# Transposes of the gate-up product tied behind later branch blocks, a last up stage in two branches, and paired down rows

## The chip, the cores and the metric

The kernel runs on one core of one Trainium2 chip. The metric is device time in microseconds of one execution; the median of several executions counts.

## The reference

A two-layer network on 256 tokens of width 1024, all in fp32. Layer 0 has a gated delta-rule mixer and a dense SwiGLU, layer 1 a windowed attention and a mixture of experts. The change touches the mixture alone:

```python
def moe_swiglu(x, w_router, w_gate, w_up, w_down):
    ...
    top_val, top_idx = lax.top_k(logits, TOP_K)          # TOP_K = 2 of 8 experts
    top_w = jax.nn.softmax(top_val, axis=-1)
    gates = jnp.einsum('nk,nke->ne', top_w, jax.nn.one_hot(top_idx, N_EXPERTS))
    for e in range(N_EXPERTS):
        h = jax.nn.silu(xf @ w_gate[e]) * (xf @ w_up[e])  # 1024 -> 3584
        out = out + gates[:, e:e + 1] * (h @ w_down[e])   # 3584 -> 1024
```

## The kernel before

The experts run one after another, each on up to 128 gathered tokens. An expert's 3584 hidden columns are cut into seven blocks b of 512. The weights come from HBM in units of 1 MB (128 partitions x 2048 fp32), 42 units an expert: two for each of gate, up and down of each block. `unit` (L140 to L158) issues the load on SP's queue into a ring of raw buffers, lets ScalarE cast it to the short form hi (L154) and VectorE subtract to get the rest lo (L155). There are four buffers each for hi and lo.

TensorE then multiplies. In the three-product arm (`mm3`, L167) each weight column block is used as hi with the tokens' hi and lo part and as lo with the hi part; the two-product arm (`mm2`, L1202) packs hi and lo of up to 64 tokens into one operand, uses each weight twice, and adds the halves with a matmul against `fold` (`addlow`, L1194). `arms` (L1184) puts both arms into a branch on TensorE, which takes the first when the expert has over 64 tokens; expert 0 always takes the first, with no branch. In this run experts 0, 2, 3 and 5 take three products, the others two.

The order is a list of stages (L1296 to L1302). For the blocks of an expert in groups (0, 1), (2, 3), (4, 5), (6): gate of each block, up of each block, then down of the blocks of the group before, then "held". After the last up of a group ScalarE takes silu of the gate sum into `msg`. "held" adds the halves of up in the two-product arm; its other arm is empty. `multiply` (L1327) makes msg times up on VectorE and puts the result into the list `held`; `turn_one` takes one from there to `turned` (L1250): four transposes on TensorE into a bank of `tr` (two banks), ScalarE's copy to the hi half of `hT` (L1256), VectorE's difference (L1257), and, from expert 1 on, ScalarE's two packing copies to `hp` (L1118, L1119). Down of a block reads hT in the one arm, hp in the other.

The framework orders each engine's instructions by itself: it simulates the engines and takes, of what would be ready, what was traced first. A branch block counts as one piece. `tc.issue_after(ins)` puts instructions of the engine of `ins` behind it in the order and adds no wait.

The main loop (L1333) decides where `multiply` and `turn_one` are traced: multiply after gate of an even block, but in "held" for the group (4, 5); turn_one after gate of an odd block or of block 6, and after each up. In the trace the transposes of experts 1 to 7 stand mostly directly behind the held block, between the two down blocks of a group, and those of expert 0 behind gate and up stages.

Of the kernel before, what the change touches and what calls it, by code (L numbers as in the profile page):

```python
# [30 lines left out]
P = 128  # L31
D = 1024
# [7 lines left out]
NE = 8  # L40
# [42 lines left out]
def kernel(ctx: ExitStack, tc: tile.TileContext, A, out):  # L83
    nc = tc.nc
# [12 lines left out]
    ident = per.tile([P, P], F32, name="ident")  # L97
# [42 lines left out]
    def unit(src, a, b, pieces=1):  # L140
        raw = next(raws[0])()
        n = a * b
        for c in range(pieces):
            w = slice(c * b // pieces, (c + 1) * b // pieces)
            nc.sync.dma_start(raw[:, :n].rearrange("p (a b) -> p a b", a=a)[:, :, w], src[:, :, w])
        hi = split.tile([P, 2048], F32R, name="hi", tag="hi")
        lo = split.tile([P, 2048], F32R, name="lo", tag="lo")
        nq = quanta[0]
        with ExitStack() as late:
            if behind[0] is not None:  # L150
                late.enter_context(tc.issue_after(behind[0].ins))
            for q in range(nq):
                c = slice(q * n // nq, (q + 1) * n // nq)
                S.copy(hi[:, c], raw[:, c])  # L154
                subs.append(V.tensor_sub(lo[:, c], raw[:, c], hi[:, c].bitcast(F32)))  # L155
        return (hi[:, :n].rearrange("p (a b) -> p a b", a=a), lo[:, :n].rearrange("p (a b) -> p a b", a=a))
# [931 lines left out]
    with ExitStack() as mctx:  # L1088
# [92 lines left out]
        NB = EF // 512  # L1181
        acc, flags = {}, {}
        y = []
        def arms(e, heavy, light):  # L1184
            if e == 0:
                return heavy()
            if e not in flags:
                flags[e] = nc.values_load(cntsi[0:1, e:e + 1], engines=(mybir.EngineType.PE,), min_val=0, max_val=T)
            with tc.If(flags[e] > HALF) as c:  # L1189
                heavy()  # L1190
            with c.Else():
                light()

        def addlow(ps, low):  # L1194
            PE.matmul(ps, fold, low, start=False, stop=True, skip_group_check=True)
# [8 lines left out]
            for i, w in enumerate(ws[0] + ws[1]):  # L1204
                PE.matmul(ps, x[:, (k0 + i % n) * P:(k0 + i % n + 1) * P], w, start=first and i == 0, stop=last and i == 2 * n - 1)  # L1205

        def gateup(e, b, us, ps, then=lambda: None):

            x = xg[e].rearrange("p l k c -> p l (k c)")
            nk, k0 = (4, 0) if len(ps) == 1 else (2, 4 * (b % 2))  # L1210
            first, last = (len(ps) == 1 or b % 2 == n for n in range(2))

            def parts():
                for u, ws in enumerate(us):
                    for h, p in enumerate(ps):
                        yield p, k0 + nk * u, [[w[:, k, h * 512:(h + 1) * 512] for k in range(nk)] for w in ws], \
                            first and u == 0, last and u == 1

            def heavy():
                for p, k1, (wh, wl), a, z in parts():  # L1220
                    mm3(p, lambda k: x[:, 0, (k1 + k) * P:(k1 + k + 1) * P], lambda k: x[:, 1, (k1 + k) * P:(k1 + k + 1) * P],
                        list(zip(wh, wl)), a, z)

            def light():
                for p, k1, ws, a, z in parts():
                    mm2(p, xp[e], k1, ws, a, z)
                then()
            arms(e, heavy, light)
# [20 lines left out]

        def turned(s, e):  # L1250
            p = trb()
            for f in range(4):
                PE.transpose(p[:, f * P:(f + 1) * P], s[:, f * P:(f + 1) * P], ident)  # L1253
            hT = mp.tile([P, 2, 512], F32R, name="hT", tag="hT")
            hp = mp.tile([P, 512], F32R, name="hp", tag="hp") if e else None
            S.copy(hT[:, 0], p)  # L1256
            V.tensor_sub(hT[:, 1], p, hT[:, 0].bitcast(F32))  # L1257
            if e:
                packed(hp, p, hT[:, 1])
            return hT, hp  # L1260
# [44 lines left out]
        def loads(what, e, b):  # L1305
            if what == "down":
                behind[0] = None
                v = wd_[e].rearrange("(f p) n -> p f n", p=P)
                return [unit(v[:, 4 * b + 2 * u:4 * b + 2 * u + 2, :], 2, D) for u in range(2)]
            w = (wg_ if what == "gate" else wu_)[e]  # L1310
            behind[0] = placed if (e, b) == (0, 1) or (e, b, what) == (0, 0, "up") else None
            if b == NB - 1:
                return colunits(w, 512 * b, 512)
            k0, c0 = 4 * (b % 2), 1024 * (b // 2)
            v = w.rearrange("(k p) n -> p k n", p=P)
            return [unit(v[:, k0 + 2 * u:k0 + 2 * u + 2, c0:c0 + 1024], 2, 1024) for u in range(2)]
# [6 lines left out]
        def turn_one():  # L1323
            e, b, s = held.pop(0)
            hT[e, b] = turned(s, e)

        def multiply():  # L1327
            for bb, pu, _, s_, ee in mine:
                V.tensor_mul(s_, s_, pu)  # L1329
                held.append((ee, bb, s_))  # L1330
            mine.clear()

        for what, e, b in stages:  # L1333
            if what != "held":
                nxt = next(nexts, None)
                quanta[0] = 1 if e or b > 1 else 4
                if nxt:
                    ready[nxt] = loads(*nxt)
                us = ready.pop((what, e, b))
            whole = b == NB - 1 or b % 2  # L1340
            if what == "gate":
                if b % 2 == 0:
                    pgs = [mm() for _ in range(1 if whole else 2)]
                gateup(e, b, us, pgs)
                if b % 2 == 0 and b < NB - 1:
                    multiply()
                elif held:
                    turn_one()
                if whole:
                    lgs_ = [low(p) if e else None for p in pgs]  # L1350
                if kept is not None and (e, b) == (kept[0] + 1, 2):
                    next(kept[1], None)
                    kept = None
            elif what == "up":
                if b % 2 == 0:
                    pus = [up() for _ in range(1 if whole else 2)]
                gateup(e, b, us, pus, lambda: [addlow(p, l) for p, l in zip(pgs, lgs_)] if whole else None)
                if held:
                    turn_one()
                if whole:  # L1360
                    for n, (pg, pu) in enumerate(zip(pgs, pus)):
                        s_ = mp.tile([P, 512], F32, name="msg", tag="msg")
                        S.activation(s_, pg, AF.Silu)
                        mine.append((b - len(pgs) + 1 + n, pu, low(pu) if e else None, s_, e))
                if b == 1 and e + 1 < NE:
                    fetch(e + 1)
                if b == 5 - 2 * (e > 0) and e + 1 < NE:
                    xg[e + 1] = gather(e + 1)
            elif what == "held":
                if e:  # L1370
                    arms(e, lambda: None, lambda: [addlow(pu, lu_) for _, pu, lu_, _, _ in mine])
                if b == NB - 2 or (e, b) == (NE - 1, NB - 1):
                    multiply()
                if (e, b) == (NE - 1, NB - 1):
                    turn_one()
                if (e, b) == (NE - 2, NB - 1):
                    turns.remove(ylng[0])
                    yy = per.tile([P, 2, D], F32, name="y", tag="Bh")
                    for tb in range(2):
                        y.append(yy[:, tb])  # L1380
                        nc.gpsimd.dma_start(y[tb], x3d[tb * P:(tb + 1) * P])
                        G.tensor_scalar(y[tb], y[tb], ALPHA, None, op0=OP.mult)
                if e == NE - 1 and b > 1:
                    with tc.issue_after(subs[-1].ins):
                        for c in late:
                            next(c, None)
                    late = [collect(b // 2 - 1, tb) for tb in range(2)] if b < NB - 1 else []
                    for c in late:
                        next(c)
                if (e, b) == (NE - 1, 1):  # L1390
                    turns.remove(ylng[1])
                    lnp = ln_params(3, nc.gpsimd)
                if (e, b) == (NE - 1, 5):
                    onehot(e, True)
            else:
                down(e, b, hT.pop((e, b)), us)
                if b == NB - 1 and e < NE - 1:
                    kept = (e, keep(e))
                    next(kept[1])
# [104 lines left out]
```

## Time and profile before

| | us |
|---|---|
| median of 3 runs | 1416.77 (1416.58 to 1417.6) |
| profiled execution | 1412.96 |
| its span in the trace | 1411.3 |
| the eight experts in it | about 475 to 1393 |

The page gives the busy share of each engine over the whole span. The trace can be asked for busy time by stretch (windows), for who waited for whom (waits) and for the instructions in order of time (timeline). PE is TensorE, DVE VectorE, ACT ScalarE. A matmul's end is modelled and overlaps the next one's start; the pace of matmuls is read from their starts.

### The profile page before, as it was taken

How to read it: one execution, taken by the hardware profiler on the slowest of the kernel's cores; microseconds unless marked ns; L12 is line 12 of the kernel's file. 1: busy time of each engine (PE TensorE's matmuls, PEld its weight loads, DVE VectorE, ACT ScalarE, POOL GpSimd, SP SyncE). 2: the span in 40 equal slices, each digit the busy share in tenths (PEclk: the TensorE clock that was granted, in tenths of full speed). 3: DMA queues.
4: the chain of work that ended last, by engine and by line, in shares of the span. 5: the costliest groups of instructions: out<-in, count | busy, mean ns of one | idle time of the engine just before them, and what ended most of it. 6: DMA issues, size and time to landing. Idle time of an engine off the chain costs nothing. (4 is left out here: it accounts for less than half of the span.)

```text
span 1411.3 us, 17398 instructions
## 1 busy us (share of the span) xinstructions
PE 1309.4 (93%) x6175; PEld 1042.5 (74%) x6175; DVE 1165.8 (83%) x1300; ACT 1013.4 (72%) x1264; POOL 67.3 (5%) x90
## 2 busy tenths in 40 slices
PE   7999999999999999988999999998989999888884
PEld 5889788888777888766677777776667776666662
DVE  4885975554877898889988888889998889999998
ACT  4763544444364577799888878789988888998983
POOL 4000000000000320000000000000000000002110
PEclk9999999999999899999999999999999999999998
DMA  8641576764643899999999999999999999999992
GB/s 272 199 151 61 180 260 220 236 209 151 203 174 117 306 421 415 362 397 404 419 410 378 353 368 359 359 372 409 405 419 416 357 375 380 395 414 418 419 416 80
DMA packets 145378, 446.76 MB, mean 317 GB/s; under 512 B 12704, under 2 KB 20032, under 8 KB 145264
## 3 DMA queue, kind: packets, MB, share of 16 engines
q1 hardware_dynamic: 137072, 420.64, 78.3%
q0 software_dynamic: 5280, 18.66, 3.5%
q10 hardware_dynamic: 2912, 5.90, 1.3%
q8 instruction: 76, 1.25, 0.3%
q14 instruction: 38, 0.31, 0.1%
HBM read 435.05 MB, written 15.36 MB: 319 GB/s over the span
## 5 line engine op out<-in xcount | busy, mean ns | idle before, releaser
L155 DVE TENSOR_TENSOR lo<-raw,hi 128x2048 fp32r<-128x2048 f32 (+1 forms) x610 | 910.2, 1534 | 115.8 <-ACT hi L154 111.8
L154 ACT CAST hi<-raw 128x2048 fp32r<-128x2048 f32 (+1 forms) x610 | 769.5, 1312 | 152.5 <-PE acc L171 59.1
L1205 PE MATMUL acc<-lo,xp 128*128 128x512 f32 x224 | 74.6, 420 | 18.7 <-DVE lo L155 16.4
L170 PE MATMUL acc<-hi,hT 128*128 128x512 f32 x224 | 88.4, 395 | 2.0 <-ACT hi L154 2.0
L170 PE MATMUL mm<-hi,xg 128*128 128x512 f32 x224 | 87.5, 392 | 0.5 <-ACT low L1199 0.5
L170 PE MATMUL acc<-hi,xg 128*128 128x512 f32 x224 | 88.0, 393 | 0.0
L171 PE MATMUL mm<-hi,xg 128*128 128x512 f32 x224 | 87.3, 390 | 0.0
L171 PE MATMUL acc<-hi,hT 128*128 128x512 f32 x224 | 87.3, 390 | 0.0
L171 PE MATMUL acc<-hi,xg 128*128 128x512 f32 x224 | 87.2, 389 | 0.0
L1205 PE MATMUL mm<-lo,xp 128*128 128x512 f32 x224 | 70.7, 403 | 10.2 <-DVE lo L155 10.1
L1205 PE MATMUL acc<-lo,hp 128*128 128x512 f32 x224 | 71.5, 400 | 4.5 <-DVE lo L155 4.4
L1205 PEld LDWEIGHTS acc<-lo,xp 128*128 128x128 f32 x224 | 38.8, 190 | 45.1 <-DVE lo L155 39.1
L1205 PE MATMUL acc<-hi,hp 128*128 128x512 f32 x224 | 70.7, 397 | 1.2 <-ACT hp L1119 1.2
L1205 PE MATMUL mm<-hi,xp 128*128 128x512 f32 x224 | 68.7, 393 | 2.2 <-ACT low L1199 1.5
L1205 PE MATMUL acc<-hi,xp 128*128 128x512 f32 x224 | 69.7, 398 | 0.0
L173 PE MATMUL acc<-lo,hT 128*128 128x512 f32 x224 | 69.0, 389 | 0.0
L173 PE MATMUL acc<-lo,xg 128*128 128x512 f32 x224 | 67.7, 389 | 0.0
L173 PE MATMUL mm<-lo,xg 128*128 128x512 f32 x224 | 67.7, 389 | 0.0
L1329 DVE TENSOR_TENSOR msg<-msg,acc 128x512 f32<-128x512 f32 x56 | 36.5, 684 | 36.0 <-PEq L1189 33.1
L1205 PEld LDWEIGHTS mm<-lo,xp 128*128 128x128 f32 x224 | 40.3, 188 | 27.3 <-DVE lo L155 19.9
L1118 ACT CAST hp<-tr 128x256 fp32r<-128x256 f32 x49 | 19.0, 387 | 55.0 <-DVE hT L1257 54.9
L1253 PE MATMUL tr<-ident,msg 128*128 128x128 f32 x224 | 34.9, 284 | 22.6 <-DVE msg L1329 22.6
(410 smaller groups left out, 2325.6 us busy)
## 6 DMA issues: line engine op xcount, KB each, us to landing
raw<-in_moe_w_gate_dram SPq DMA_DIRECT2D x112, 1024.0 KB, 7.8
raw<-in_moe_w_up_dram SPq DMA_DIRECT2D x112, 1024.0 KB, 7.5
raw<-in_moe_w_down_dram SPq DMA_DIRECT2D x112, 1024.0 KB, 8.0
raw<-in_a_w_in_dram SPq DMA_DIRECT2D x12, 1024.0 KB, 5.6
raw<-in_ffn_w_gate_dram SPq DMA_DIRECT2D x11, 1024.0 KB, 5.0
raw<-in_ffn_w_up_dram SPq DMA_DIRECT2D x11, 1024.0 KB, 5.1
raw<-in_ffn_w_down_dram SPq DMA_DIRECT2D x11, 1024.0 KB, 4.9
raw<-in_b_w_in_dram SPq DMA_DIRECT2D x5, 1024.0 KB, 5.1
```

The costliest lines, as they stand in the source:

```text
L154: S.copy(hi[:, c], raw[:, c])
L155: subs.append(V.tensor_sub(lo[:, c], raw[:, c], hi[:, c].bitcast(F32)))
L170: PE.matmul(ps, xh(k), wh, start=first and k == 0, stop=False)
L171: PE.matmul(ps, xl(k), wh, start=False, stop=False)
L173: turn[0] = PE.matmul(ps, xh(k), wl, start=False, stop=last and k == n - 1)
L1118: S.copy(v[:, :, 0], p)
L1205: PE.matmul(ps, x[:, (k0 + i % n) * P:(k0 + i % n + 1) * P], w, start=first and i == 0, stop=last and i == 2 * n - 1)
L1253: PE.transpose(p[:, f * P:(f + 1) * P], s[:, f * P:(f + 1) * P], ident)
L1329: V.tensor_mul(s_, s_, pu)
```

## The change

Four edits. `arms` notes the end of the stage's branch block (for expert 0 its last matmul), and `turned` ties its transposes behind it. `multiply` moves to "held" for every group, and turn_one is now traced after gate of an odd block and after up of an even block. For block 6 the up stage is cut into its two units, each a branch block of its own (expert 0: no branch), with a turn_one after each. Down weights are loaded with two adjoining rows to a partition, 8 KB in one piece instead of two pieces of 4 KB; the transposes take every second column of the product to match.

```diff
+        stage_end = [None]
+
         def arms(e, heavy, light):
             if e == 0:
-                return heavy()
+                heavy()
+                stage_end[0] = turn[0].ins
+                return
...
             with c.Else():
                 light()
+            stage_end[0] = nc.cur_bb.bb.instructions[-1]
...
-        def gateup(e, b, us, ps, then=lambda: None):
+        def gateup(e, b, us, ps, then=lambda: None, only=(0, 1)):
...
-                for u, ws in enumerate(us):
+                for u in only:
+                    ws = us[u]
...
             p = trb()
-            for f in range(4):
-                PE.transpose(p[:, f * P:(f + 1) * P], s[:, f * P:(f + 1) * P], ident)
+            pairs = s.rearrange("t (u p k) -> t u k p", u=2, k=2)
+            with tc.issue_after(stage_end[0]):
+                for f in range(4):
+                    PE.transpose(p[:, f * P:(f + 1) * P], pairs[:, f // 2, f % 2], ident)
...
-                v = wd_[e].rearrange("(f p) n -> p f n", p=P)
-                return [unit(v[:, 4 * b + 2 * u:4 * b + 2 * u + 2, :], 2, D) for u in range(2)]
+                v = wd_[e].rearrange("(g p k) n -> p g k n", p=P, k=2)
+                return [unit(v[:, 2 * b + u], 2, D) for u in range(2)]
...
-                if b % 2 == 0 and b < NB - 1:
-                    multiply()
-                elif held:
+                if held and b % 2:
                     turn_one()
...
-                gateup(e, b, us, pus, lambda: [addlow(p, l) for p, l in zip(pgs, lgs_)] if whole else None)
-                if held:
-                    turn_one()
+                then = lambda: [addlow(p, l) for p, l in zip(pgs, lgs_)] if whole else None
+                if b == NB - 1:
+                    for u in range(2):
+                        gateup(e, b, us, pus, then if u else lambda: None, (u,))
+                        if held:
+                            turn_one()
+                else:
+                    gateup(e, b, us, pus, then)
+                    if held and b % 2 == 0:
+                        turn_one()
...
-                if b == NB - 2 or (e, b) == (NE - 1, NB - 1):
-                    multiply()
+                multiply()
```

## Rows read from the trace of the kernel before

**Rows 1.** Part 1 of the page: engine, busy us (share), instructions.

```profile
PE 1309.4 (93%) x6175; PEld 1042.5 (74%) x6175; DVE 1165.8 (83%) x1300; ACT 1013.4 (72%) x1264; POOL 67.3 (5%) x90
```

**Rows 2.** Windows, experts 0 to 5 and 7: length, busy us per engine, clock, DMA share, GB/s.

```profile
475.00:588.00 113.00, 113.00 (x517) 93.48 (x516) 104.04 (x101) 87.70 (x91) 17.59 (x9) 1.00 0.98 389
588.00:695.50 107.50, 94.62 (x399) 70.43 (x398) 100.02 (x57) 96.37 (x92) 1.07 (x2) 0.98 1.01 397
695.50:818.50 123.00, 118.89 (x536) 96.96 (x535) 105.91 (x61) 100.85 (x97) 1.07 (x2) 1.00 0.98 380
818.50:942.80 124.30, 119.99 (x541) 97.89 (x541) 103.89 (x59) 99.97 (x95) 1.07 (x2) 1.00 0.96 364
942.80:1049.30 106.50, 94.02 (x396) 68.61 (x395) 101.39 (x57) 97.65 (x92) 1.07 (x2) 1.00 1.02 410
1049.30:1172.10 122.80, 118.69 (x536) 96.78 (x535) 105.74 (x61) 100.79 (x97) 1.07 (x2) 1.00 0.99 381
...
1278.60:1393.00 114.40, 97.72 (x401) 69.59 (x399) 112.53 (x72) 98.12 (x93) 13.47 (x9) 1.00 0.91 371
```

**Rows 3.** TensorE's waits, experts 2 and 3: waiter, releaser, us, times, longest.

```profile
PE tr L1253 <- DVE msg L1329: 7.5, 8, 0.9
```

**Rows 4.** VectorE's waits, all experts.

```profile
DVE lo L155 <- ACT hi L154: 43.8, 87, 2.2
DVE msg L1329 <- PEq L1189: 33.1, 12, 3.8
DVE lo L155 <- DMA raw<-in_moe_w_gate_dram: 0.6, 1, 0.6
```

**Rows 5.** ScalarE's waits, all experts.

```profile
ACT hp L1118 <- DVE hT L1257: 54.9, 35, 4.1
ACT hT L1256 <- PE tr L1253: 22.1, 16, 2.6
```

**Rows 6.** Timeline, TensorE, expert 2: start, us, line, tiles, count [idle before].

```profile
787.01 0.61 PE L173 MATMUL acc<-lo,hT 128*128 128x512 f32 x2
788.57 1.25 PE L1253 MATMUL tr<-ident,msg 128*128 128x128 f32 x8 [0.94 <-DVE msg L1329]
789.58 0.47 PE L170 MATMUL acc<-hi,hT 128*128 128x512 f32 x1
```

**Rows 7.** Timeline, VectorE, the same place.

```profile
787.83 1.28 DVE L1329 TENSOR_TENSOR msg<-msg,acc 128x512 f32<-128x512 f32 x2 [3.77 <-PEq L1189]
789.03 4.49 DVE L155 TENSOR_TENSOR lo<-raw,hi 128x2048 fp32r<-128x2048 f32 x2
793.43 0.69 DVE L1257 TENSOR_TENSOR hT<-tr,hT 128x512 fp32r<-128x512 f32 x1
```

**Rows 8.** Timeline, TensorE, last held block of expert 2.

```profile
812.57 0.66 PE L1253 MATMUL tr<-ident,msg 128*128 128x128 f32 x4 [0.94 <-DVE msg L1329]
```

**Rows 9.** Timeline, TensorE, expert 0, block 6: gate to up to down.

```profile
570.81 0.60 PE L1253 MATMUL tr<-ident,msg 128*128 128x128 f32 x4
571.16 0.48 PE L170 MATMUL acc<-hi,xg 128*128 128x512 f32 x1
...
577.09 0.48 PE L170 MATMUL acc<-hi,hT 128*128 128x512 f32 x1
```

**Rows 10.** Timeline, VectorE, the same place.

```profile
574.25 0.68 DVE L1257 TENSOR_TENSOR hT<-tr,hT 128x512 fp32r<-128x512 f32 x1
```

**Rows 11.** Timeline, TensorE, expert 2, border of two gate blocks at 701.17.

```profile
700.71 0.62 PE L173 MATMUL mm<-lo,xg 128*128 128x512 f32 x2
701.17 0.39 PE L170 MATMUL mm<-hi,xg 128*128 128x512 f32 x1
```

**Rows 12.** Timeline, ScalarE, start of expert 1.

```profile
592.35 0.59 ACT L1256 CAST hT<-tr 128x512 fp32r<-128x512 f32 x1 [2.60 <-PE tr L1253]
```

**Rows 13.** Timeline, VectorE, the same place.

```profile
592.97 0.69 DVE L1257 TENSOR_TENSOR hT<-tr,hT 128x512 fp32r<-128x512 f32 x1 [0.90 <-ACT hT L1256]
594.78 4.49 DVE L155 TENSOR_TENSOR lo<-raw,hi 128x2048 fp32r<-128x2048 f32 x2 [1.12 <-ACT hi L154]
```

## The prediction

> **What bounds the kernel now.** I read four views in this order. Part 1 of the page first: TensorE is busy 93% of the span, VectorE 83%, ScalarE 72% [rows 1]. As an average that names nothing, so second the windows, one for each of the eight experts that fill 475 to 1393 us [rows 2]; expert 6's row repeats expert 4's and is left out. The reader should see two kinds there. Experts 0, 2, 3 and 5 take 113 to 124.3 us with TensorE busy 97 to 100%: they run the three-product arm and TensorE sets their pace. Experts 1, 4, 6 and 7 take 106.5 to 114.4 us with VectorE busy 93 to 98% and TensorE only 85 to 88%: they run the two-product arm, and VectorE's 42 splits set the pace, with ScalarE close behind (90 to 92% in experts 1, 4 and 6). What a saved TensorE stall is worth depends on which kind it lies in.
>
> Third the waits. In experts 2 and 3 TensorE's one large wait is that of the transposes for the product msg: 7.5 us in 8 places [rows 3]. VectorE waits 33.1 us in 12 places for PEq at L1189, that is for the branch block of stage "held", before it can make msg [rows 4]. Neither list has a DMA of any weight: VectorE waited 0.6 us for one in all experts together [rows 4], and ScalarE's list has none.
>
> Fourth the timeline at one such place in expert 2. The last matmul of the first down block starts at 787.24 (two from 787.01, 0.23 apart), so the next could start at 787.47. VectorE starts msg only at 787.83, since it stood waiting for the empty branch block [rows 7]; the eight transposes come at 788.57, and the second down block at 789.58 [rows 6]. TensorE lost 2.11 us from 787.47 on, for work that nobody needs before the next group's down stages.
>
> **The change part by part.** Expert 0 has no branch, and its transposes already stand where the change puts most of the others, behind a gate or an up stage: four start at 570.81 and the next matmul at 571.16 with no wait, 0.35 us a set [rows 9]. I take that as the price of a set anywhere.
>
> Gain, experts 2, 3 and 5. Each has three places with two sets: 2.11 - 2 x 0.35 = 1.41 us each. Expert 3's first one and both light-to-heavy crossings have a further short wait for a ScalarE copy; I leave it. The fourth place has one set and waits 0.94 us [rows 8]. So 3 x 1.41 + 0.94 = 5.2 us an expert, 15.5 us for three.
>
> What is late next. VectorE still gets its release only when TensorE reaches the held block, and then makes two products (1.28 us) and splits the last down unit until 789.03 + 4.49 / 2 = 791.28 [rows 7]. TensorE, now at the second down block at 787.47, wants that unit's lo 16 matmuls later: 787.47 + 16 x 0.23 = 791.15. It would wait 0.13 us, or 0.3 with the semaphore; before, it came to that point 2.11 us later. 0.3 x 9 places = 2.7 us back. Nothing else is queued on TensorE that could fill it.
>
> The multiply, traced in "held" always: it stands for the same seven operations an expert, 0.68 us each, on an engine that in experts 2, 3, 5 idles 17 to 20 us [rows 2]. The one behind it on VectorE is the next split; its wait for the branch is there already. Price 0; if it lands earlier in VectorE's order, the wait grows, and I allow the 0.3 above a second time (2.7 us) in the range.
>
> The last up stage in two branches. The transposes of the fourth and fifth blocks move from the down stages before into and behind the up stage of block 6, and down of block 4 follows at once. From the first set to that down there are now 12 matmuls and two sets: 12 x 0.23 + 0.35 = 3.1 us to its first matmul. What the set must go through first is seen in expert 0: transposes at 570.81, difference on VectorE at 574.25 for 0.68 us, so hT is there 4.12 us after [rows 9, 10]. Expert 0 does not notice, as its down starts at 577.09, 6.3 us after. With 3.1 us it would stall 1.0 us. Bounds: 0, if both engines stand ready (0.60 transposes, 0.59 copy, 0.68 difference are 1.9 us, under 3.1), and 2.4, if two splits lie before the difference as in expert 2 (789.58 - 1.01 to 793.43 + 0.69: 5.5 us after the set) [rows 6, 7]. I take 1.0, as expert 0 is the nearest, for the four TensorE-bound experts: 4.0 us. In the light ones TensorE has 12 us to spare an expert.
>
> The seven added branches: at a border of two blocks (701.17, gate of block 0 to block 1) matmuls follow one another 0.23 us apart as within a block [rows 11]. Price 0. The Trainium skill (Runtime: NRT & Kernel Launch, Instruction fetch mechanics) speaks against this: a taken branch out of the prefetched pages makes the engine wait for a fetch. The row shows no such wait at this border; were it to come at the new ones, see the rivals.
>
> Two adjoining down rows: 112 of the 336 expert loads get 8 KB instead of 4 KB a partition in one piece. No engine waits for these loads [rows 4], so a faster one is worth 0. A slower one is hidden up to the reading ahead; the bound from rows: expert 1 moved 397 GB/s, expert 4 410 [rows 2], 3% apart, and 3% of a 106.5 us expert's third is 1.1 us, which four light experts might show: 4 us in the range, either way.
>
> The transposes now read every second column of msg. No row here has such a read. Bounds: 0, and a doubled set (0.35 more). I take 0 as all other transposes of the trace, contiguous ones, follow the matmuls without a gap. By the Trainium skill (SBUF — State Buffer, Door 1) steps of up to four fp32 within a 16-byte line cost nothing; no run here shows it yet.
>
> Light experts (1, 4, 6, 7): the stalls that go were TensorE's, which has slack; VectorE keeps its operations. It idles 5 to 7.5 us in experts 1, 4 and 6, mostly for ScalarE's hi (43.8 us in 87 places over all experts) [rows 2, 4], and ScalarE waits for the difference hT before packing (54.9 us in 35 places) [rows 5]; both chains stay. With a set move its copy and two packs on ScalarE and its difference on VectorE, at unchanged counts; no DMA changes its place on SP's or POOL's queue. Price 0, with 2 us an expert either way.
>
> **Sum.** 15.5 - 2.7 - 4.0 = 8.8 us of 1412.96 (the profiled execution; its span is 1411.3). The median of the runs shown is 1416.77, 3.8 above; the difference lies outside the changed work, so I take 8.8 from the median: 1408.0. Beyond 0.2%, about 2.8 us, a measurement of this kernel can tell a difference.
>
> **Rivals.**
> B, better: the chain after the new up halves is short (0 instead of 4.0), the lo is not late (0 instead of 2.7), the light experts gain their 2 us each: 1408.0 - 14.7 = 1393 at the end, 1399 in the middle. For it: copies and differences had VectorE and ScalarE waiting ahead of TensorE in experts 2 and 3 [rows 5, 7]. Against: ScalarE is at 90% in the light ones.
>
> C, cancelled: every set in the TensorE-bound experts costs twice as much, for the stride or for a wait in its new place: 28 x 0.35 = 9.8, so 1417.8, no change. For: nothing in the trace shows such reads. Against: the gapless sets of expert 0.
>
> D, slower: ScalarE, in order, stands at the copy of hT until TensorE has come through the block that the set is now tied behind, and the hi casts behind it, and so VectorE's splits, come late where VectorE is the bound. There is one light place before with a set behind a gate block: at 591.72 in expert 1 the copy waited 2.60 us [rows 12], and VectorE lost 0.90 and then 1.12 us [rows 13], 2.02 together. With that at half of the 28 sets of the light experts: 14 x 2.02 = 28.3, so 1436. It decides from 8.8 / 28 = 0.31 us a set. Against: this place is where an expert of the other kind ends, when ScalarE is farthest ahead; deeper in, it is about one unit ahead and would find the set done.
>
> E, branches fetch: each of the seven new borders stalls TensorE. The nearest price is the one wait behind an outside instruction, 0.94 us [rows 8]: 6.6 us, so 1414.6, still lower than before in the median, within 0.2%. Beside it stands the rule of the skill's runtime page named above.
>
> **How the numbers follow.** Forecast 0.55 (1402 to 1412 as its own range), B 0.16, C 0.09, D 0.14, E 0.06. Faster is the forecast and B less a small part of the forecast's upper end, 0.70; the same is C, E and that part, 0.15; slower is D and a little of C, 0.15. The range leaves out D and the far end of B: 1396 to 1420.
>
> **What would show it.** In the changed trace: no wait of TensorE for msg in experts 2, 3 and 5, and 2.1 us less from down to down; experts 2, 3, 5 about 3.5 to 5 us shorter each, expert 0 about 1 us longer, light ones within 2 us. A TensorE wait of about 1 us for hT before down of block 4 shows the price of the last up stage; sets longer than 0.35 us show C; a larger ScalarE wait for tr and VectorE idle in experts 1, 4, 6, 7 show D; gaps at the border inside the last up stage show E. It is wrong if the light experts move more than the others, or if the down loads change what any engine waits for.

## The result, and the profile after

| | before | after |
|---|---|---|
| median, us | 1416.67 (1412.97 to 1417.6) | 1501.74 (1496.36 to 1506.91) |
| ratio, 95% interval | | 1.061 [1.057, 1.065] |
| span of the profiled execution | 1411.3 | 1505.2 |

The change makes the kernel 85 us slower; forecast were 8.8 us the other way, and the time lies far above the range.

Part 1 of the page of after: engine, busy us (share), instructions.

```profile
PE 1341.6 (89%) x6175; PEld 1058.8 (70%) x6175; DVE 1171.9 (78%) x1300; ACT 1009.6 (67%) x1264; POOL 67.9 (5%) x90
```

Beside [rows 1] the work of VectorE and ScalarE is the same to 6 us; what grew by some 94 us is the span, so the loss of these two is waiting. TensorE's busy time grew by 32 us, though it issues as many instructions.

Windows of after, experts 1 to 6, each from one expert's first gate matmuls to the next one's: length, busy us per engine, clock, DMA share, GB/s.

```profile
592.50:711.90 119.40, 98.67 (x396) 72.39 (x395) 100.90 (x57) 96.40 (x92) 1.07 (x2) 0.96 0.96 359
711.90:846.40 134.50, 122.90 (x536) 97.67 (x535) 105.75 (x60) 100.18 (x96) 1.07 (x2) 0.99 0.92 343
846.40:982.70 136.30, 124.30 (x541) 98.75 (x540) 104.48 (x59) 98.97 (x95) 1.07 (x2) 0.99 0.90 332
982.70:1103.20 120.50, 97.69 (x396) 71.24 (x395) 102.70 (x58) 96.94 (x94) 1.07 (x2) 0.97 0.97 369
1103.20:1237.90 134.70, 123.16 (x536) 97.55 (x535) 105.80 (x60) 100.35 (x96) 1.06 (x2) 0.99 0.91 342
1237.90:1358.30 120.40, 97.81 (x395) 71.32 (x394) 102.74 (x58) 96.91 (x94) 4.81 (x4) 0.97 0.97 363
```

Against [rows 2] each of experts 1 to 6 is 11.5 to 14 us longer, whichever arm it runs (expert 1 107.5 to 119.4, 2 123.0 to 134.5, 3 124.3 to 136.3, 4 106.5 to 120.5); expert 0, whose copies and sets were not pushed behind a branch block, took 113.2 us as against 113.0. VectorE's idle time, the length less its busy time, went in expert 1 from 7.5 to 18.5, in 2 from 17.1 to 28.8, in 3 from 20.4 to 31.8, in 4 from 5.1 to 17.8: it grew by 11.0 to 12.7 us in each, nearly all that was lost.

Who waits for whom in the whole of after (waiter, releaser, us, times, longest), ScalarE's largest line, VectorE's two largest, then TensorE's in experts 2 and 3 alone.

```profile
ACT hT L1264 <- PE tr L1261: 157.4, 45, 7.2
DVE lo L155 <- ACT hi L154: 161.5, 135, 3.8
DVE hT L1265 <- ACT hT L1264: 46.4, 33, 4.2
...
PE acc L173 <- DVE lo L155: 10.9, 12, 1.1
PE tr L1147 <- ACT hp L1118: 5.6, 2, 2.8
PE acc L170 <- PEq L1193: 2.3, 4, 0.7
```

ScalarE's wait for the transposes rose from 22.1 us in 16 places [rows 5] to 157.4 in 45. The wait for msg, the largest of TensorE in experts 2 and 3 before [rows 3], is gone, and in its place TensorE waits for VectorE's lo.

One such place in expert 2, timelines of after in the order ScalarE, VectorE, TensorE: start, duration, instruction, count, and in brackets the idle time before it and who ended it.

```profile
787.17 1.92 ACT L154 CAST hi<-raw 128x2048 fp32r<-128x2048 f32 x1 [1.71 <-PE mm L171]
795.35 0.59 ACT L1264 CAST hT<-tr 128x512 fp32r<-128x512 f32 x1 [6.26 <-PE tr L1261]
795.84 1.91 ACT L154 CAST hi<-raw 128x2048 fp32r<-128x2048 f32 x1
...
785.70 6.69 DVE L155 TENSOR_TENSOR lo<-raw,hi 128x2048 fp32r<-128x2048 f32 x3
795.97 0.69 DVE L1265 TENSOR_TENSOR hT<-tr,hT 128x512 fp32r<-128x512 f32 x1 [3.58 <-ACT hT L1264]
797.78 2.29 DVE L155 TENSOR_TENSOR lo<-raw,hi 128x2048 fp32r<-128x2048 f32 x1 [1.12 <-ACT hi L154]
...
794.23 0.62 PE L173 MATMUL mm<-lo,xg 128*128 128x512 f32 x2
794.69 0.63 PE L1261 MATMUL tr<-ident,msg 128*128 128x128 f32 x4
795.07 0.47 PE L170 MATMUL acc<-hi,xg 128*128 128x512 f32 x1
...
800.13 0.73 PE L173 MATMUL acc<-lo,xg 128*128 128x512 f32 x2 [1.12 <-DVE lo L155]
```

This is the case in one picture. The set stands on TensorE behind the gate block, at 794.69. ScalarE's next instruction, from 789.09 on, is the copy of that set; it stands there 6.26 us and casts nothing, while TensorE works without a gap through a block whose weights are ready. VectorE runs dry at 792.39 and stands behind ScalarE for 3.58 and 1.12 us. Then TensorE, 16 matmuls into the next block, waits for lo, 1.12 us. It has run ahead on finished weights while the makers of the next ones waited for it.

### The profile page after: what moved, and what is told of

The parts are those of the page before. It is cut to its first block, busy times and chain, and to the rows that moved or that the text cites. A ratio compares the mean times of both kernels' runs of the same rounds, so it can differ in the third digit from the quotient of the medians.

```text
span 1505.2 us, 17335 instructions
## 1 busy us (share of the span) xinstructions
PE 1341.6 (89%) x6175; PEld 1058.8 (70%) x6175; DVE 1171.9 (78%) x1300; ACT 1009.6 (67%) x1264; POOL 67.9 (5%) x90
## 5 line engine op out<-in xcount | busy, mean ns | idle before, releaser
L1264 ACT CAST hT<-tr 128x512 fp32r<-128x512 f32 x56 | 32.9, 587 | 157.4 <-PE tr L1261 157.4
L170 PE MATMUL acc<-hi,xg 128*128 128x512 f32 x224 | 91.7, 409 | 0.0
L171 PE MATMUL acc<-hi,xg 128*128 128x512 f32 x224 | 89.4, 399 | 0.0
L1210 PE MATMUL acc<-hi,xp 128*128 128x512 f32 x224 | 78.5, 439 | 6.2 <-ACT hi L154 5.9
L173 PE MATMUL acc<-lo,xg 128*128 128x512 f32 x224 | 71.1, 405 | 13.4 <-DVE lo L155 13.4
L1210 PEld LDWEIGHTS acc<-lo,xp 128*128 128x128 f32 x224 | 43.5, 205 | 54.5 <-DVE lo L155 46.1
L1265 DVE TENSOR_TENSOR hT<-tr,hT 128x512 fp32r<-128x512 f32 x56 | 38.6, 690 | 46.4 <-ACT hT L1264 46.4
L1210 PEld LDWEIGHTS acc<-lo,hp 128*128 128x128 f32 x224 | 40.1, 189 | 36.8 <-DVE lo L155 29.8
```

What stands on the lines that cost most here:

```text
L170: PE.matmul(ps, xh(k), wh, start=first and k == 0, stop=False)
L171: PE.matmul(ps, xl(k), wh, start=False, stop=False)
L173: turn[0] = PE.matmul(ps, xh(k), wl, start=False, stop=last and k == n - 1)
```

## The experiments

Each run is given against the kernel before on the same chip. "Middle" and "end" in the text are worked out from the starts of VectorE's splits in the timelines: 610 in each kernel, counted from the last one back in groups of 42, one group for an expert (a group starts with the second gate block of its expert). How much later split n starts than split n of before is taken at a group's 7th and 35th split; the growth between is the expert's middle, and from the 35th to the next one's 7th its end. In the change a middle holds the sets of blocks 0 to 3 and an end those of blocks 4 to 6. In the kernel before, and where the sets stand behind the last down block, the double place of blocks 4 and 5 comes earlier and lies in the middle too.

| us lost against before | middles of experts 1, 2, 3, 4, 5, 6, 7 | seven ends together |
|---|---|---|
| after | 8.9, 6.0, 6.2, 8.5, 6.2, 8.5, 10.5 | 34.7 |
| no tie | 1.6, 0.2, 0.2, 0.1, 0.2, 0.1, 0.1 | 0.7 |
| copy behind one more cast | 3.3, -2.6, -2.5, 1.4, -2.6, 2.8, 3.6 | 23.4 |
| copy a stage later | -2.1, 0.9, 1.0, 1.2, 0.9, 1.2, 3.5 | 42.5 |
| copy a stage later, up whole | -0.6, -0.1, 0.1, 1.0, 0.0, 1.0, 3.4 | 37.8 |
| blocks 4, 5 untied | 4.3, -1.6, -1.4, 2.4, -1.4, 2.4, 4.5 | 8.6 |
| blocks 4, 5, 6 untied | 2.4, 0.4, 0.5, 2.4, 0.5, 2.4, 4.1 | 0.6 |
| sets behind the last down block | 4.9, 3.0, 3.0, 3.3, 3.2, 3.2, 3.6 | 4.0 |
| the same, copy behind one more cast | 0.0, -0.4, -0.2, 1.8, -0.4, 1.9, 2.9 | 19.1 |

**Which edit.** Without the tie, all else changed:

```diff
-            with tc.issue_after(stage_end[0]):
-                for f in range(4):
...
+            for f in range(4):
...
```

> The changed kernel without the tie: the transposes are free to be ordered anywhere again, the rest of the change stays (moved multiply and turn_one, last up stage in two branches, paired rows). Theory (the tie puts the transposes behind a whole gate or up block, and ScalarE, in order, stands at the copy of hT with the hi casts behind it): the time falls back to within 1% of before, 1405 to 1425 us, and ScalarE's wait for the transposes falls from 157 us to under 40. Rival 1 (paired rows or the strided transposes cost the time): stays near 1500. Rival 2 (the last up stage in two branches costs it): stays above 1450.

1417.2 us, ratio 1.002 [1.001, 1.004]. The tie alone on the kernel before (`arms` notes the block's end, `turned` is tied behind it, nothing else):

> The kernel before with the tie alone: transposes behind the end of the latest branch block, multiply, turn_one, up stage and rows as before. Theory: most of the loss comes with the tie alone, 1470 to 1510 us, ScalarE waits over 120 us for the transposes. Rivals 1 and 2: within 1% of before.

1498.3, ratio 1.060 [1.055, 1.064]. The paired rows and the strided transposes alone on the kernel before:

> The kernel before with the paired down rows and the strided transposes alone. Theory: no engine waits for these loads, so 1412 to 1420 us; a set of four transposes up to 0.04 us longer. Rival 1: 1480 or more.

1416.0, ratio 1.0015 [1.000, 1.003]. So the tie is the loss, whole; the other three edits without it are worth 0.2%. (Without it the framework brings the instructions almost into the order of before: ScalarE's differs in the place of one cast, TensorE's in that of one set and one down matmul. So this run doesn't tell what the moved calls would cost in another order.) ScalarE's waits, of the kernel without the tie and of that with the tie alone:

```profile
ACT hp L1118 <- DVE hT L1264: 54.3, 35, 4.1
ACT hT L1263 <- PE tr L1260: 23.6, 16, 2.6
...
ACT hT L1262 <- PE tr L1259: 149.9, 42, 6.2
```

The first two answer to the 54.9 and 22.1 us of [rows 5]; the third comes with the tie.

**The last up stage.** The change with this stage whole and both turns behind it:

> The changed kernel with the last up stage whole and both turns of its group behind it; the tie stays. Theory: the tie's cost stays, so 1480 to 1510 us. Rival 2 (the split last up is the cost): near 1417.

1509.1, ratio 1.068 [1.064, 1.071]. That is 7 us over the change's median, but the two intervals overlap and the profiled spans are alike (1505.2 us both), so no difference is shown. With the sets tied, the cut, which I charged with 4.0 us, shows no cost here.

**Is it ScalarE's standing?** If it is, the sets can stay tied where the copies stand deeper in ScalarE's and VectorE's order. The change with the copy, the difference and the packs behind the newest traced cast and split, which puts one more unit ahead of them:

```diff
-            S.copy(hT[:, 0], p)
...
+            with tc.issue_after(casts[-1].ins), tc.issue_after(subs[-1].ins):
+                S.copy(hT[:, 0], p)
...
```

> The changed kernel, whole, and besides the copy of hT tied on ScalarE behind the latest hi cast traced and its difference on VectorE behind the latest split, so that one more unit is ready before ScalarE stands at the copy. Theory: the wait for the transposes stays but starves nobody in the three-product experts: at least half of the loss comes back, 1410 to 1460 us. If the loss were TensorE's or the loads' own, the time would stay within 1% of 1500.

1448.7, ratio 1.024 [1.022, 1.027]: 53 of 85 us are back, with these sets where the change has them (TensorE's order differs from the change's only in the place of the transposes of the next expert's tokens). The middles of experts 2, 3 and 5 are now 2.5 to 2.6 us shorter than before; TensorE's wait for msg, which I had forecast to go, is gone there. What is left lies at the ends. One of them (end of expert 1), TensorE's timeline in this run, then ScalarE's and VectorE's:

```profile
691.38 0.63 PE L1262 MATMUL tr<-ident,msg 128*128 128x128 f32 x4
695.71 1.22 PE L1211 MATMUL acc<-hi,hp 128*128 128x512 f32 x2 [3.69 <-ACT hp L1120]
696.73 1.05 PE L1211 MATMUL acc<-lo,hp 128*128 128x512 f32 x2
```

```profile
689.94 0.61 ACT L1266 CAST hT<-tr 128x512 fp32r<-128x512 f32 x1
...
694.98 0.37 ACT L1119 CAST hp<-tr 128x256 fp32r<-128x256 f32 x1 [0.54 <-DVE hT L1267]
...
683.25 11.09 DVE L156 TENSOR_TENSOR lo<-raw,hi 128x2048 fp32r<-128x2048 f32 x5
694.26 1.28 DVE L1267 TENSOR_TENSOR hT<-tr,hT 128x512 fp32r<-128x512 f32 x2
```

Down of block 4 follows the second set at once and waits 3.69 us for hp. ScalarE had copied the set of block 4 at 689.94 already; its difference stands on VectorE behind five splits until 694.26, and the packs, which need it, come at 694.98. So it is VectorE's queue, in which the edit put the difference deeper too, that makes hp late.

Then the same idea a whole stage later: the copies are traced when the next stage is, behind that stage's casts (the transposes stay where the change has them).

> The changed kernel with the ScalarE and VectorE half of turned (copy of hT, difference, packing) traced one stage later, behind the hi casts of that stage's load: some three units ahead of TensorE instead of one or two. Theory: ScalarE no longer stands at the copy, its wait for the transposes falls from 157 us (80 with one more unit) to under 30, the two-product experts come back to 106 to 109 us and the time to 1405 to 1425. If ScalarE's place is not what costs the rest, it stays near 1449.

1476.4, ratio 1.044 [1.042, 1.047]: a miss, 50 us over what I expected. And with the last up stage whole, its turns behind gate and up of block 6:

> As e5_copy_late, and the last up stage whole again, with the two turns of that group after gate and up of block 6. Theory: the split last up costs under 1.5 us an expert, so 5 to 12 us less than e5_copy_late, about 1403 to 1415. Rival (the split costs nothing): within 3 us of e5_copy_late.

1465.7, ratio 1.036 [1.034, 1.039], 10.7 us less. And with the transposes of the next expert's tokens tied behind the branch block too, from expert 2 on:

> As e6_late_whole, and the transposes of the next expert's tokens, from expert 2 on, tied behind the up block of block 3, so that they find free tr banks. Theory: the wait of 2.8 us for the packing copies in each expert goes; TensorE-bound experts gain up to 2.8 us each, 3 to 9 us less than e6_late_whole. If that wait is hidden, no difference.

1465.6, ratio 1.036 [1.032, 1.039], no difference. The table shows where the miss lies: with the copies a stage later and the up stage whole the middles are back to within 1 us in experts 1 to 6 and lose 3.4 in the last, and the ends cost 37.8 (42.5 with the up stage cut). TensorE's largest wait in the run of 1465.7 us, and ScalarE's:

```profile
PE acc L1211 <- ACT hp L1120: 29.1, 8, 4.7
...
ACT hp L1119 <- DVE hT L1270: 78.0, 46, 6.4
```

ScalarE no longer stands at the copy; it stands ahead of the packs, 78.0 us for VectorE's difference as against 54.9 in [rows 5], and TensorE waits for their outcome. In the middles one or two stages lie between a set and its down, at the ends none.

**Ends as before.** Copy behind one more cast, last up whole, and the sets of blocks 4 and 5 free of every tie; this is the edit of the first of two runs, and in the second the first line leaves out block 6 too:

```diff
+            tied = b in (0, 1, 2, 3, 6)
+            with tc.issue_after(stage_end[0]) if tied else ExitStack():
...
```

> The changed kernel with the cast tied ahead of the copy (as in the run that gave 1448.7 us), but the last up stage whole, and the sets of the fourth and fifth blocks (b = 4, 5) tied neither on TensorE nor on ScalarE and VectorE, as in the kernel before; the other 39 sets stay tied. Theory 1 (what is left of the loss in that run, some 30 us, arises at the ends of the experts, where down of block 4 follows its transposes at once and waits up to 3.7 us for hp): the ends come back, the time is 1413 to 1423. Theory 2 (what is left is spread over all tied sets): five of seven sets still pay, 1435 to 1445. Rival: ScalarE's order of the untied sets suffers from the tied ones and it is as slow as with the ends tied, 1446 to 1452.

1434.3, ratio 1.014 [1.012, 1.016], above what my theory gave and just under the other's.

> As the run beside it, but the set of block 6 (turned behind gate of block 1 of the next expert) is untied too; the sets of blocks 0 to 3 stay tied. Theory 1: 1412 to 1420, at or below the run beside it, since nothing at an expert's end is tied any more; three heavy experts keep 2 of 3 double places free of the wait for msg, worth up to 3 x 2 x 1.4 = 8.5 us less the late lo and the bare block border. Theory 2 (spread): 1428 to 1440. Rival: the set of block 6 is where a tie costs nothing, no difference beyond 2 us to the run beside it.

1424.0, ratio 1.007 [1.005, 1.009], between the two theories; the rival, no difference between these two runs, is out by 10 us. The ends cost 8.6 and then 0.6 us: untied, they are as before. But the middles, which I took to be free, cost 12.7 together in the second run: 2.4 in each of experts 1, 4 and 6 (1.6 of the first are there without any tie, too), 4.1 in the last, 0.4 to 0.5 in the others. There ScalarE still waits 41.8 us for transposes in 23 places, as against 22.1 in 16 before:

```profile
ACT hT L1270 <- PE tr L1263: 41.8, 23, 4.4
```

By the timeline the surplus lies at one set: 23.5 us in seven places are the copy of block 2, once in each of experts 1 to 7 (before 3.6 us in three); at the others it waits as before. Both of my theories were half right: the loss has a part at the ends and a part in the middles.

**The smallest step.** The kernel before, where from expert 1 on each set is tied behind the last down block, so that the double sets come just after that block and not just ahead of it; ScalarE's and VectorE's programs are, instruction for instruction, those of before:

```diff
-            for f in range(4):
...
+            with tc.issue_after(down_end[0]) if e else ExitStack():
+                for f in range(4):
...
```

> The kernel before with one edit: from expert 1 on each set is tied behind the branch block of the last down stage, so that the double sets stand after the second down block of their group in place of ahead of it; ScalarE's and VectorE's programs keep the order of the kernel before. Theory (ScalarE stands at the copy for as long as TensorE is late with the set): TensorE comes one down block later with it, at most 5.7 us, the copy had some lead, and each double place costs VectorE 0 to 3 us in the light experts, against a gain of at most 1.41 - 0.55 us at 9 places of the heavy experts (7.7 us): 1408 to 1430, where 1418 would say that both cancel. Rival 1 (only the distance of two or three stages hurts, one block is within ScalarE's lead): the gain alone, 1405 to 1410, faster than before. Rival 2 (any tie to a branch block costs the framework's order): over 1440.

1444.1, ratio 1.021 [1.020, 1.023]. My first rival, that one block lies within ScalarE's lead, is out. The time lies 14 us above the theory's range and in that of the second rival, but the rival's reason does not hold: no order but TensorE's has changed. Here the cause can be seen with nothing else changed. The same double set in the light expert 1, of before (ahead of it TensorE's row of the set) and then of this run, first ScalarE's rows, then VectorE's:

```profile
670.58 1.26 PE L1253 MATMUL tr<-ident,msg 128*128 128x128 f32 x8 [0.69 <-DVE msg L1329]
...
668.00 3.74 ACT L154 CAST hi<-raw 128x2048 fp32r<-128x2048 f32 x2
671.61 0.62 ACT L1256 CAST hT<-tr 128x512 fp32r<-128x512 f32 x1
...
675.43 0.69 DVE L1257 TENSOR_TENSOR hT<-tr,hT 128x512 fp32r<-128x512 f32 x1
```

```profile
668.74 3.79 ACT L154 CAST hi<-raw 128x2048 fp32r<-128x2048 f32 x2
676.27 0.59 ACT L1260 CAST hT<-tr 128x512 fp32r<-128x512 f32 x1 [3.75 <-PE tr L1257]
...
676.89 0.69 DVE L1261 TENSOR_TENSOR hT<-tr,hT 128x512 fp32r<-128x512 f32 x1 [0.60 <-ACT hT L1260]
678.70 4.67 DVE L155 TENSOR_TENSOR lo<-raw,hi 128x2048 fp32r<-128x2048 f32 x2 [1.12 <-ACT hi L154]
```

Before, ScalarE comes to the copy at 671.61 and finds the set done, with no idle time ahead of it, and so no visible lead either. One down block later it stands 3.75 us, and VectorE, which had been ahead by the two splits of its queue, loses 0.60 and 1.12 us: of the 3.75 us 1.72 get through to it. TensorE's own down block in turn waits for a lo, at the double set before this one (TensorE, the same run):

```profile
642.80 0.74 PE L1207 MATMUL acc<-lo,hp 128*128 128x512 f32 x2 [1.19 <-DVE lo L155]
643.38 0.62 PE L1207 MATMUL acc<-hi,hp 128*128 128x512 f32 x2
643.84 0.62 PE L1207 MATMUL acc<-lo,hp 128*128 128x512 f32 x2
644.30 1.03 PE L1257 MATMUL tr<-ident,msg 128*128 128x128 f32 x8
```

In before this block, which stands behind the set, has no such wait; it starts after TensorE's 0.70 us for msg. The lo that the block lacks delays the set behind it, and the set's copy delays the next hi and lo. As I read these rows, the three engines wait for one another in turn.

The same with the copies behind one more cast:

> As the run beside it, with the copy and difference of each set but those of block 6 tied behind the newest traced cast and difference, so that one or two casts more stand ahead of the copy on ScalarE. Theory: ScalarE no longer stands at the copy, the light experts give nothing up in the middle, and what the run beside it loses there comes back: 1406 to 1415. Rival (the copy is then late for down of block 4, as in the run that gave 1448.7 us with a wait of 3.7 us for hp): 4 to 6 us in each of 7 experts, 1430 to 1450.

1442.6, ratio 1.021 [1.019, 1.023], no gain in all: the middles come back (24.2 to 5.6 us, all seven), the ends go from 4.0 to 19.1. That is where the rival had the loss, but not by its reason: TensorE waits for hp once, 2.9 us. ScalarE's wait for the transposes, and the last place of expert 1:

```profile
ACT hT L1265 <- PE tr L1258: 32.3, 8, 6.1
...
695.78 0.59 ACT L1265 CAST hT<-tr 128x512 fp32r<-128x512 f32 x1 [2.76 <-PE tr L1258]
```

All eight are the set of block 6, one in each expert, whose copy this run leaves where it was; behind that of expert 1 VectorE's splits start 2.0 us later. The run with the copies unmoved stands there too (30.6 us), so what else makes these ends dearer stays open. No version beats the kernel before; the best of those with a tie gives up 0.7%.

## Why the prediction was wrong

**The step that failed** is that on the light experts: "With a set move its copy and two packs on ScalarE and its difference on VectorE, at unchanged counts ... Price 0". Counts and busy times did stay; what changed is where an engine that runs in order stands while it waits: ScalarE's wait at the copies grew from 22.1 to 157.4 us, and VectorE's idle time by 11.0 to 12.7 us in each expert shown. The same step is missing for the experts bound by TensorE, where I counted VectorE's 17 to 20 us of idle time as a cushion for the moved multiply. For a late copy it is none, since a copy that stands holds up the casts behind it, whatever the average.

**Rival D** named this mechanism, and its price was nearly right. At 2.02 us a set, seven sets in seven experts would make 49 x 2.02 = 99 us; measured were 85 (94 between the spans), 1.7 to 1.9 a set. That the average comes so near is partly luck, as it takes together light and TensorE-bound experts, gains at msg and TensorE's slower clock. Wrong was its scope: I gave it half of the light experts' sets, 14 of 49. The argument against it, that ScalarE "is about one unit ahead and would find the set done", could have been refuted from the trace of before: the row at 671.61 shows ScalarE reaching the copy with the set just done (the transposes start there at 670.58), so a set that comes later lets it stand. One down block later 1.72 us of that reached VectorE, over D's own turning point (0.31 us a set). By the Trainium skill (PSUM — Partial Sum Buffer, Engine vs sequencer instructions) the queues of ScalarE and VectorE are strict FIFO; the 6.26 us at the copy agree, as the cast behind it waits too and then starts with no wait of its own (795.84).

**The gain on the msg stalls.** The stalls did go. Where the copy did not stand in the way, the middles of experts 2, 3 and 5 got 2.5 to 2.6 us shorter (run of 1448.7 us); my terms give 3 x (1.41 - 0.3) = 3.3 for the three double places of before that lie in a middle. So this term was some three quarters of its size, in a kernel other than the one forecast. One item was missing: the block border behind "held". Before, TensorE's waits list none for PEq; I take it that the msg stall hid it. In after TensorE waits 11 times for PEq, 0.54 to 0.70 us each, together 6.3 us; this is one, the first matmul behind such a border:

```profile
1131.40 0.49 PE L170 MATMUL mm<-hi,xg 128*128 128x512 f32 x1 [0.55 <-PEq L1193]
```

**The late lo**, 0.3 us at 9 places, was 12 places in experts 2 and 3 alone, 10.9 us. It was worked out with VectorE's and ScalarE's start as before; it is the outlet of the failed step. The 0.3 in it was 0.13 and 0.17 for a semaphore, and no run shows the latter: in the picture above the split ends at 800.07 and TensorE starts at 800.13, 0.06 us.

**The last up stage in two**, charged with a wait for hT of 1.0 us in each TensorE-bound expert: expert 0 is 0.2 us longer, and TensorE's waits in experts 2 and 3 have no hT among them. Undoing it shows no clear difference in the change and gives 10.7 us where the copies come a stage later. The sum also left out one of the two sets; with it there are 3.46 us to the down block, not 3.1. What held is my lower bound, both engines ready: in expert 2 VectorE and ScalarE stood empty at this set, so its difference was done 1.97 us after the set began, and down of block 4 (833.00) found it there.

```profile
829.37 0.63 PE L1261 MATMUL tr<-ident,msg 128*128 128x128 f32 x4
830.65 0.69 DVE L1265 TENSOR_TENSOR hT<-tr,hT 128x512 fp32r<-128x512 f32 x1 [3.08 <-ACT hT L1264]
833.00 0.47 PE L170 MATMUL acc<-hi,hT 128*128 128x512 f32 x1
```

**Branches** at 0: none of the 11 waits for PEq stands at the border inside the last up stage, so E is out. **Rows and stride** at 0: the run with these alone is within 0.2%, its down loads land after 8.1 us (before 8.0), and a set of strided transposes takes 0.38 us (794.69 to 795.07 above) as against 0.35 [rows 9], 0.03 x 56 = 1.7 us at most; C's doubled set is out. The Trainium skill (SBUF — State Buffer, Door 1) would have this step for nothing; the set shows the 0.03 us.

**What stays open.** The last 10 us of the run at 1424.0 (2.4 us in each light middle, 4.1 in the last expert) go with waits of ScalarE for the set of block 2, but no run takes them away with the tie in place. In the change, ScalarE's and VectorE's own orders differ from before as well; with nothing but TensorE's order changed 29 of the 85 us are shown, and how the rest divides between standing and order is not. TensorE's busy time in after, 32 us over before, is only partly explained by its clock (below) and by the first matmul behind each wait.

## What to carry to other kernels

Before an instruction is moved later on one engine, look up its first consumer on every other engine and read the idle time ahead of it: where that is nil or follows the producer at once, the consumer has no lead, and what stands behind it in its queue moves by the delay until some idle time takes it up. A stall that is taken from one engine by ordering its work later is a gain only if the consumers move back in their queues by as much, and that again only if what they make is not due at once. Idle time of an engine that feeds others in order is no cushion for a single instruction of it.

## What the runs showed of the hardware

TensorE's clock fell after a wait. In the run of 1448.7 us, windows ahead of the 3.69 us wait for hp, behind it, and after that (length, busy per engine, clock, DMA share, GB/s):

```profile
685.00:691.00 6.00, 5.88 (x27) 4.30 (x26) 6.00 (x4) 5.55 (x5) 0.00 (x0) 1.00 1.02 406
695.70:702.20 6.50, 6.49 (x16) 5.09 (x17) 2.04 (x1) 5.19 (x7) 0.00 (x0) 0.52 1.03 423
702.40:706.00 3.60, 2.81 (x13) 2.04 (x12) 3.15 (x3) 3.50 (x2) 0.00 (x0) 1.00 0.46 193
```

The granted clock was 0.52, the lower level of 1.2 GHz, over these 6.5 us; 16 matmuls took 6.49 us, where at the full clock 13 take 2.81 (0.22 each), so the wait of 3.69 us cost some 3 us more behind it. The mean clock over the span was 0.988 before and 0.973 in after. As an estimate from these means, TensorE spent some 34 and 81 us at the lower level; 47 us more at half the pace are at most 24 of the 32 us that its busy time grew.
